# Later modulations summed on VectorE, and neighbourhood queries and keys projected straight into transposed form

## The chip, the cores and the metric

The kernel runs on one core of one Trainium2 chip. The metric is device time in microseconds (us) of one execution, as the median of several runs. One further execution was taken with the hardware profiler; all durations below are from that one.

## The reference, cut to what matters

Two layers of a diffusion backbone work on 1024 latent tokens and 256 context tokens, with a model width of 1024. In each layer a conditioning vector gives shift, scale and gate, the normalised input is modulated and projected once, four branches mix the tokens (A neighbourhood attention, B latent attention, C a recurrent scan, D grouped-query attention), and the branches are merged and projected. Everything is float32. Two places matter here:

```python
def modulation(cond, w_mod, b_mod):
    mod = jax.nn.silu(cond) @ w_mod + b_mod          # (1024,) @ (1024, 3072)
    return jnp.split(mod, 3, axis=-1)                # shift, scale, gate
...
p_lat = (layer_norm(x) * (1.0 + scale) + shift) @ w_in
q, k, v = (split_heads(tt, NA_HEADS) for tt in lat[0:3])    # branch A: 256 columns each
```

The modulation is a vector times a matrix, done for two conditions (latent and context) and for both layers. Branch A's queries and keys are the first 512 columns of the combined projection.

## The kernel before, in words

Data is held in tiles of 128 partitions. The 1280 tokens (256 context, then 1024 latent) make ten token tiles. The modulated input lies transposed in on-chip memory as `xh` and `xl` (width on the partitions, tokens along the free axis), split into a high and a low part of the reduced float type `fp32r`; a float32 product is three `fp32r` products, high x high, high x low and low x high (`mm_a`, `mm_b`, lines 302 to 317). Weights are split in the same way when they are loaded: ScalarE casts the high part (line 263), VectorE subtracts it to get the low part (line 264).

The work of one layer runs in this order: the projection of D (`g_proj`), then two streams woven together, one with the projections of B and A (`m_proj`, `a_proj`) and one with the recurrent branch C (`lru`), then the three attentions (`g_att`, `m_att`, `a_att`) with parts of the gates' products woven in, then `merge`, and then the output projection and the norm (`last`, `outp`). In the profile's names a prefix such as `a_proj__` or `merge__` is the stage, and `wide` is a PSUM tile of three banks that several stages share.

`weave` (line 80) takes generators with a weight each and always advances the one that is least far along for its weight; a generator's `yield` ends one step. A tile framework then sets the final order on each engine's queue and adds the waits, so steps that stand side by side in the code can be interleaved finely. Each engine works its queue in order. SyncE (SP) issues the loads and ScalarE's queue the stores of the projections.

**Modulation.** `modulation` (line 170) loads a piece of `w_mod` of 128 rows and 512 columns (line 185), and multiplies it in float32 with the 128x2 tile `sc` (the two conditions) as the stationary operand and the weights as the moving operand (line 188). The result for 256 or 512 columns lies on two partitions, one group of columns in each of four 32-partition groups of one PSUM bank. At the end ScalarE copies the rows out (line 194), TensorE turns them with small transposes (line 197), and VectorE adds the bias (line 199). The first modulation is needed at the kernel's start. The three later ones (gate of layer 0, shift and scale of layer 1, gate of layer 1; `later_mods`, line 1165) are 64 pieces in all. They are woven with the merge of layer 0 (line 1011): 96 steps of the merge against a weight of 68 for the modulations, which have 67 steps.

**Merge.** For each of the four branches and each of eight output blocks c, `merge` (line 979) forms the gate's product (24 matmuls for a group of tokens, even c) or loads one formed earlier (odd c), applies a sigmoid on ScalarE (line 999), forms the branch's product (6 matmuls into a bank of `wide`), multiplies the two on VectorE (line 1005) and adds the result to the accumulator on VectorE for even c and on GpSimd for odd c (line 1006). In layer 0 there are three groups of tokens (256, 512 and 512), in layer 1 two of 512. The loads of the modulation's pieces use three rotating buffers (tag `q`).

**Projection of A.** `a_steps` (line 801) forms, for each token tile, 24 matmuls with the tokens as the stationary operand and the 512 weight columns as the moving one, so that tokens come out on the partitions. ScalarE copies the two halves out of PSUM, the queries scaled by 0.125 (lines 808 and 809). `put_t` (line 341) then turns the tile with four transposes on TensorE (line 348), splits it into high and low (lines 312 and 313), and stores both in the scratch tensor `qk_a` with two DMAs whose inner runs are 128 tokens (512 bytes). For layer 1 the two context tiles need no queries and use 256 columns. The values follow with weights of their own (lines 819 to 822). The two PSUM banks of `ps_mm` are used in turn.

## Time and profile before

| | |
|---|---|
| median of three runs | 2924.19 us (2923.29 to 2927.37) |
| the profiled execution's own time | 2926.0 us |
| its span, first to last instruction | 2924.2 us |
| TensorE (PE) busy | 2782.2 us, 95% of the span |
| VectorE (DVE) busy | 1503.1 us, 51% |
| ScalarE (ACT) busy | 1219.3 us, 42% |
| GpSimd (POOL) busy | 420.1 us, 14% |
| mean granted TensorE clock | 0.979 of full speed |
| merge of layer 0 with the modulations | about 1085 to 1477 us |
| projection of A woven with the recurrent branch | about 259 to 410 us and 1821 to 1957 us |

An engine's busy time is the time in which at least one of its instructions runs. Matmuls are pipelined, so that a matmul's duration is longer than its distance to the next one; what it costs TensorE is read from the distance between starts. PEld is the load of a stationary operand, which can run beside a matmul.

### The profile page before, as it was taken

How to read it: one execution, taken by the hardware profiler on the slowest of the kernel's cores; microseconds unless marked ns; L12 is line 12 of the kernel's file. 1: busy time of each engine (PE TensorE's matmuls, PEld its weight loads, DVE VectorE, ACT ScalarE, POOL GpSimd, SP SyncE). 2: the span in 40 equal slices, each digit the busy share in tenths (PEclk: the TensorE clock that was granted, in tenths of full speed). 3: DMA queues.
4: the chain of work that ended last, by engine and by line, in shares of the span. 5: the costliest groups of instructions: out<-in, count | busy, mean ns of one | idle time of the engine just before them, and what ended most of it. 6: DMA issues, size and time to landing. Idle time of an engine off the chain costs nothing. (4 is left out here: it accounts for less than half of the span.)

```text
span 2924.2 us, 40179 instructions
## 1 busy us (share of the span) xinstructions
PE 2782.2 (95%) x14458; PEld 2248.4 (77%) x14458; DVE 1503.1 (51%) x3085; ACT 1219.3 (42%) x2617; POOL 420.1 (14%) x507
## 2 busy tenths in 40 slices
PE   7978999999999999999999797999999999999998
PEld 4766788888888887777767586788888888777776
DVE  5645435555455652233358655445555556533357
ACT  4353535445455552222224435535545455522230
POOL 1211011110111100111222121011111111001131
PEclk9988999999999999999999898999999999999999
DMA  7424232222223324333332333342222333222232
GB/s 249 119 66 146 79 103 84 85 85 85 92 86 124 103 94 128 100 121 120 122 89 87 99 102 102 105 122 87 85 88 78 113 115 110 93 87 88 89 113 88
DMA packets 240424, 301.83 MB, mean 103 GB/s; under 512 B 27488, under 2 KB 160096, under 8 KB 240224
## 3 DMA queue, kind: packets, MB, share of 16 engines
q1 hardware_dynamic: 134368, 225.58, 24.5%
q10 hardware_dynamic: 105856, 73.68, 8.1%
q8 instruction: 114, 1.87, 0.3%
q14 instruction: 86, 0.70, 0.1%
HBM read 217.11 MB, written 82.07 MB: 102 GB/s over the span
## 5 line engine op out<-in xcount | busy, mean ns | idle before, releaser
L307 PE MATMUL merge__mm<-xh,merge__whi 128*128 128x512 f32 (+1 forms) x640 | 242.2, 378 | 0.9 <-ACT a_att__tmp L934 0.9
L308 PE MATMUL merge__mm<-xl,merge__whi 128*128 128x512 f32 (+1 forms) x640 | 238.6, 373 | 0.0
L309 PE MATMUL merge__mm<-xh,merge__wlo 128*128 128x512 f32 (+1 forms) x640 | 238.5, 373 | 0.0
L313 DVE TENSOR_TENSOR m_att__pl<-m_att__t,m_att__ph 128x384 fp32r<-128x384 f32 (+1 forms) x248 | 122.0, 508 | 117.5 <-ACT m_att__ph L312 78.8
L1005 DVE TENSOR_TENSOR merge__tmp<-wide,merge__tmp 128x512 f32<-128x512 f32 (+1 forms) x120 | 76.5, 637 | 194.8 <-PE wide L309 173.7
L263 ACT CAST merge__whi<-merge__wraw 128x256 fp32r<-128x256 f32 (+1 forms) x128 | 65.8, 514 | 249.3 <-PE merge__mm L308 172.9
L1006 POOL TENSOR_TENSOR merge__acc<-merge__acc,merge__tmp 128x512 f32<-128x512 f32 (+1 forms) x60 | 79.0, 1317 | 574.8 <-DVE merge__tmp L1005 574.7
L313 DVE TENSOR_TENSOR g_att__pl<-g_att__t,g_att__ph 128x384 fp32r<-128x384 f32 (+1 forms) x228 | 112.8, 515 | 88.3 <-ACT g_att__ph L312 56.0
L312 ACT CAST m_att__ph<-m_att__t 128x384 fp32r<-128x384 f32 (+1 forms) x248 | 105.2, 440 | 115.0 <-PE m_att__t L584 105.3
L307 PEld LDWEIGHTS merge__mm<-xh,merge__whi 128*128 128x128 f32 x640 | 120.2, 188 | 42.8 <-issue 16.5
L264 DVE TENSOR_TENSOR merge__wlo<-merge__wraw,merge__whi 128x256 fp32r<-128x256 f32 (+1 forms) x128 | 72.0, 563 | 131.8 <-ACT merge__whi L263 124.8
L309 PEld LDWEIGHTS merge__mm<-xh,merge__wlo 128*128 128x128 f32 x640 | 120.3, 188 | 23.8 <-issue 0.4
L308 PEld LDWEIGHTS merge__mm<-xl,merge__whi 128*128 128x128 f32 x640 | 120.3, 188 | 22.4
L307 PE MATMUL wide<-merge__uh,merge__whi 128*128 128x256 f32 (+1 forms) x320 | 127.9, 400 | 9.3 <-DVE merge__tmp L1005 6.7
L312 ACT CAST g_att__ph<-g_att__t 128x384 fp32r<-128x384 f32 (+1 forms) x228 | 98.2, 446 | 83.3 <-PE g_att__t L584 78.7
L307 PE MATMUL a_att__mm<-xh,a_att__whi 128*128 128x512 f32 (+1 forms) x320 | 123.7, 387 | 0.0
L641 DVE TENSOR_SCALAR_CACHE_REDUCE g_att__p<-wide 128x1280 f32<-128x1280 f32 (+1 forms) x72 | 98.6, 1369 | 45.9 <-PE wide L639 35.7
L641 DVE TENSOR_SCALAR_CACHE_REDUCE m_att__p<-wide 128x1280 f32<-128x1280 f32 (+1 forms) x72 | 98.7, 1371 | 42.3 <-PE wide L639 41.8
L309 PE MATMUL a_att__mm<-xh,a_att__wlo 128*128 128x512 f32 (+1 forms) x320 | 120.0, 377 | 0.0
L308 PE MATMUL a_att__mm<-xl,a_att__whi 128*128 128x512 f32 (+1 forms) x320 | 120.0, 375 | 0.0
L308 PE MATMUL wide<-merge__ul,merge__whi 128*128 128x256 f32 (+1 forms) x320 | 119.7, 374 | 0.0
L299 PE MATMUL a_proj__mm<-a_proj__whi,xh 128*128 128x256 f32 (+1 forms) x320 | 110.3, 346 | 9.9 <-ACT a_proj__whi L263 9.8
(418 smaller groups left out, 7908.4 us busy)
## 6 DMA issues: line engine op xcount, KB each, us to landing
merge__wraw<-in_w_chunks_dram SPq DMA_DIRECT2D x64, 256.0 KB, 2.9
mod__wm<-in_w_mod_dram SPq DMA_DIRECT2D x64, 256.0 KB, 3.1
g_proj__wm<-in_w_mod_dram SPq DMA_DIRECT2D x16, 512.0 KB, 9.6
a_att__wraw<-in_w_chunks_dram SPq DMA_DIRECT2D x32, 256.0 KB, 2.8
merge__wraw<-in_w_branch_dram SPq DMA_DIRECT2D x64, 128.0 KB, 2.0
merge__tmp<-start__gates SPq DMA_DIRECT2D x32, 256.0 KB, 3.2
merge__tmp<-outp__gates SPq DMA_DIRECT2D x32, 256.0 KB, 3.4
g_att__wraw<-in_w_chunks_dram SPq DMA_DIRECT2D x28, 256.0 KB, 2.7
```

The costliest lines, as they stand in the source:

```text
L263: act.copy(hi[:, :n], raw[:, :n])
L264: (pool if by_pool else dve).tensor_sub(lo[:, :n], raw[:, :n], hi[:, :n])
L299: pe.matmul(ps, xh, wh[:, n0:n1], start=first and k == 0, stop=False)
L307: pe.matmul(ps, wh, xh, start=first and k == 0, stop=False)
L308: pe.matmul(ps, wh, xl, start=False, stop=False)
L309: pe.matmul(ps, wl, xh, start=False, stop=last and k == nk - 1)
L312: act.copy(hi, src)
L313: dve.tensor_sub(lo, src, hi)
L641: dve.tensor_scalar(pt[:, :nk], wide[:, :nk], -scale, None, ALU.mult, ALU.min, accum_out=nb)
L1005: dve.tensor_mul(sgm[:, :g[1]], pb[:, :g[1]], sgm[:, :g[1]])
L1006: (pool if w is None else dve).tensor_add(acc[c][:, gs], acc[c][:, gs], sgm[:, :g[1]])
```

## The change

Two parts, and two weights of `weave` that follow the new numbers of steps.

- `later_mods` calls a new function, `modulation_apart`. For each piece of 128 rows and 512 columns, VectorE multiplies it by the condition's value of each row and adds it to a running sum, once for each of the two conditions (one `tensor_scalar` for the first of eight pieces, `scalar_tensor_tensor` for the others). After eight pieces there are two sums of 128x512. TensorE then adds up the 128 partitions: for each 128 columns a float32 matmul has the sum as its 128x128 stationary operand and one column of -0.5 as its moving operand, which puts the result on the partitions, where it is needed. VectorE multiplies by -2 and adds the bias. The rows, their copies and the small transposes are gone. The running sums lie in buffers of the tags `ph` and `pl`. The steps become 75, the weight 76. The first modulation is as it was.
- `a_steps` makes the 128x128 weight blocks the stationary operand and the tokens the moving one, so that queries and keys come out transposed. ScalarE makes the high part straight from PSUM, VectorE the low part straight from PSUM, and both are stored with inner runs of 256 or 512 tokens. The copies and transposes are gone. There are twelve pieces of work in layer 0 and ten in layer 1; the last two run side by side through the eight weight pairs, as the last two token tiles did before. The weight `W_A` goes from 30 to 32.

```diff
--- before.py
+++ after.py
@@ -34,7 +34,7 @@
 G_LAG = 1
 X_ACT = (0, 2)
 M_ORDER = (2, 3, 1, 0)
-W_A = 30
+W_A = 32
 W_B = 48
 Z_0, GATE_0 = 2, 10
 UNITS = [(2, 3), (5, 3), (8, 2)]
@@ -199,6 +199,39 @@
         dve.tensor_tensor(mc[:, :, :n].rearrange("p s n -> p n s"),
                           tps[:, :2 * n].rearrange("p (n s) -> p n s", s=2),
                           bm[:, :n, None].to_broadcast([128, n, 2]), ALU.add)
+        if n == 16:
+            dve.tensor_scalar(mc[:, :, 8:16], mc[:, :, 8:16], 1.0, None, ALU.add)
+        out["m"] = mc
+        yield
+
+    def raw_w():
+        return tp.tile([128, 512], F32, tag="q", name=nm("wm"), bufs=3)
+
+    def modulation_apart(l, base, ncols, out):
+
+        acc = ps_v.tile([128, 512], F32, tag="pv", name=nm("pm"))
+        n = ncols // 128
+        bm = lc.tile([128, 16], F32, tag="bm", name=nm("bm"))
+        sp.dma_start(bm[:, :n], a["b_mod"][l, :, base // 128:base // 128 + n])
+        for h in range(ncols // 512):
+            sums = [tp.tile([128, 512], F32, tag=tag, name=nm("ms"), bufs=b) for tag, b in (("ph", 3), ("pl", 2))]
+            for k in range(KC):
+                w = raw_w()
+                sp.dma_start(w, a["w_mod"][l, k * 128:(k + 1) * 128, base + h * 512:base + (h + 1) * 512])
+                for s in range(2):
+                    if k == 0:
+                        dve.tensor_scalar(sums[s], w, sc[:, k, s:s + 1], None, ALU.mult)
+                    else:
+                        dve.scalar_tensor_tensor(sums[s], w, sc[:, k, s:s + 1], sums[s], ALU.mult, ALU.add)
+                yield
+            for s in range(2):
+                for c in range(4):
+                    o = s * n + 4 * h + c
+                    pe.matmul(acc[:, o:o + 1], sums[s][:, c * 128:(c + 1) * 128], mhalf[:, 0:1], start=True, stop=True)
+            yield
+        mc = lc.tile([128, 2, 16], F32, tag="modc", name=nm("modc"), bufs=4)
+        dve.scalar_tensor_tensor(mc[:, :, :n], acc[:, :2 * n].rearrange("p (s n) -> p s n", s=2), -2.0,
+                                 bm[:, None, :n].to_broadcast([128, 2, n]), ALU.mult, ALU.add)
         if n == 16:
             dve.tensor_scalar(mc[:, :, 8:16], mc[:, :, 8:16], 1.0, None, ALU.add)
         out["m"] = mc
@@ -800,18 +833,35 @@
 
         def a_steps():
             wa = load_rows(w_in, C_A, 512)
-            prev = None
-            for t, ps in project(wa, lambda t: 0 if t >= q0t else 256, 512):
-                c0 = 0 if t >= q0t else 256
-                y = tmp()
-                if c0 == 0:
-                    act.activation(y[:, :256], ps[:, :256], AF.Copy, scale=0.125)
-                act.copy(y[:, 256:], ps[:, 256:])
-                if prev:
-                    put_t(*prev)
-                prev = qk_a, t, c0 // 128, [y[:, c:c + 128] for c in range(c0, 512, 128)]
+            items = [(c, g) for c in range(4) for g in (qgroups if c < 2 else groups)]
+
+            def part(c, g, ps, ks):
+                xs = xs_g(g)
+                ws = [(wh[:, c * 128:(c + 1) * 128], wl[:, c * 128:(c + 1) * 128]) for wh, wl in wa]
+                mm_b(ps[:, :g[1]], [ws[k] for k in ks], lambda j: xs(ks[j]), ks[0] == 0, ks[-1] == KC - 1)
+
+            def keep(c, g, ps):
+                n, scale = g[1], 0.125 if c < 2 else 1.0
+                hi = tp.tile([128, 512], F32R, tag="ph", name=nm("th"), bufs=3)
+                lo = tp.tile([128, 512], F32R, tag="pl", name=nm("tl"), bufs=2)
+                act.activation(hi[:, :n], ps[:, :n], AF.Copy, scale=scale)
+                dve.scalar_tensor_tensor(lo[:, :n], ps[:, :n], scale, hi[:, :n], ALU.mult, ALU.subtract)
+                for d, s in enumerate((hi, lo)):
+                    act.dma_start(qk_a[d, c, :, g[0]:g[0] + n], s.bitcast(F32)[:, :n])
+
+            for c, g in items[:-2]:
+                ps = mm()
+                part(c, g, ps, list(range(KC)))
+                keep(c, g, ps)
                 yield
-            put_t(*prev)
+
+            last = [(c, g, mm()) for c, g in items[-2:]]
+            for k in range(KC):
+                for c, g, ps in last:
+                    part(c, g, ps, [k])
+            for c, g, ps in last:
+                keep(c, g, ps)
+                yield
             wv = load_rows(w_in, C_AV, 256)
             for t, ps in project(wv, lambda t: 0, 256):
                 put_v(v_a, t, ps[:, :256].rearrange("p (h e) -> p h e", e=64))
@@ -1008,7 +1058,7 @@
 
         for _ in fill["gen"]:
             pass
-        weave((f"merge{l}", merge(), 4 * KC * len(qgroups)), (f"mod{l}", side, 68))
+        weave((f"merge{l}", merge(), 4 * KC * len(qgroups)), (f"mod{l}", side, 76))
 
 
         phase[0] = f"last{l}"
@@ -1159,13 +1209,10 @@
     ctx.push(pools)
     x1 = dr.tile([SEQ, D], F32, name="x1", bufs=1)
 
-    def raw_w():
-        return tp.tile([128, 512], F32, tag="q", name=nm("wm"), bufs=3)
-
     def later_mods():
-        yield from modulation(0, 2048, 1024, gate0, raw_w, 512)
-        yield from modulation(1, 0, 2048, mc1, raw_w, 512)
-        yield from modulation(1, 2048, 1024, gate1, raw_w, 512)
+        yield from modulation_apart(0, 2048, 1024, gate0)
+        yield from modulation_apart(1, 0, 2048, mc1)
+        yield from modulation_apart(1, 2048, 1024, gate1)
 
     def fin0(t, Y, later):
         if t >= CT:
```

## Rows read from the trace of the kernel before

**Rows 1.** The page, part 1: busy time, share of the span, instructions.
```profile
PE 2782.2 (95%) x14458; PEld 2248.4 (77%) x14458; DVE 1503.1 (51%) x3085; ACT 1219.3 (42%) x2617; POOL 420.1 (14%) x507
```

**Rows 2.** Windows: length, busy time of each engine (instructions), granted clock, DMA share, GB/s.
```profile
280.00:360.00 80.00, 80.00 (x389) 65.22 (x388) 31.05 (x34) 40.33 (x62) 0.53 (x1) 0.99 0.28 81
...
1085.00:1475.00 390.00, 385.18 (x1914) 286.72 (x1912) 138.30 (x239) 107.84 (x227) 54.02 (x48) 1.00 0.39 119
1840.00:1960.00 120.00, 115.09 (x636) 97.12 (x637) 48.35 (x64) 52.50 (x88) 0.60 (x2) 0.99 0.33 96
```

**Rows 3.** TensorE's waits from 1060 to 1480 us: total us, times, longest.
```profile
PE wide L307 <- DVE merge__tmp L1005: 3.2, 5, 0.8
PE mod__t L197 <- ACT mod__tmp L194: 1.1, 1, 1.1
...
PE mod__pm L188 <- DMA mod__wm<-in_w_mod_dram: 0.3, 1, 0.3
```

**Rows 4.** Groups of TensorE's instructions, 1085 to 1475 us: busy, mean ns, idle before.
```profile
L188 PE MATMUL mod__pm<-mod__wm,sc 128*2 128x512 f32 x64 | 21.5, 592 | 0.0
...
L188 PE MATMUL mod__pm<-mod__wm,sc 128*2 128x256 f32 x128 | 18.1, 378 | 0.3 <-DMA mod__wm<-in_w_mod_dram 0.3
...
L197 PE MATMUL mod__t<-ident,mod__tmp 2*128 2x2 f32 x28 | 3.1, 203 | 1.2 <-ACT mod__tmp L194 1.1
```

**Rows 5.** Timeline of TensorE in the merge of layer 0: start us, duration us, instruction.
```profile
1233.55 0.28 PE L308 MATMUL wide<-merge__ul,merge__whi 128*128 128x256 f32 x1
1233.67 0.28 PE L309 MATMUL wide<-merge__uh,merge__wlo 128*128 128x256 f32 x1
1233.88 1.02 PE L188 MATMUL mod__pm<-mod__wm,sc 128*2 128x512 f32 x2
1234.83 0.50 PE L307 MATMUL merge__mm<-xh,merge__whi 128*128 128x512 f32 x1
1235.17 0.39 PE L308 MATMUL merge__mm<-xl,merge__whi 128*128 128x512 f32 x1
...
1094.91 0.39 PE L308 MATMUL wide<-merge__ul,merge__whi 128*128 128x512 f32 x1
1095.13 0.39 PE L309 MATMUL wide<-merge__uh,merge__wlo 128*128 128x512 f32 x1
1095.45 0.60 PE L188 MATMUL mod__pm<-mod__wm,sc 128*2 128x256 f32 x4
1095.98 0.50 PE L307 MATMUL merge__mm<-xh,merge__whi 128*128 128x512 f32 x1
1096.32 0.40 PE L308 MATMUL merge__mm<-xl,merge__whi 128*128 128x512 f32 x1
...
1103.14 1.03 PE L188 MATMUL mod__pm<-mod__wm,sc 128*2 128x256 f32 x10
```

**Rows 6.** Groups of VectorE's instructions, whole span: busy, mean ns, idle before.
```profile
L1077 DVE SCALAR_TENSOR_TENSOR outp__Y<-outp__Y,outp__mv,outp__ln_g 128x512 f32<-128x512 f32 x36 | 25.6, 748 | 0.4
...
L313 DVE TENSOR_TENSOR a_proj__tl<-a_proj__t,a_proj__th 128x512 fp32r<-128x512 f32 x18 | 12.3, 683 | 40.6 <-ACT a_proj__th L312 40.5
...
L532 DVE TENSOR_TENSOR_SCAN lru__lruo<-lru__lrug,lru__lruo,lru__lrug 128x1024 f32<-128x1024 f32 x4 | 9.4, 2346 | 0.1
```

**Rows 7.** By tile, stationary loads, matmuls, store issues: ns min/median/max, first and last start.
```profile
L348 PEld LDWEIGHTS a_proj__t<-ident,a_proj__tmp x76: 137/140/226, 278.2 to 1926.9; 128*128 128x128 f32 x76
L348 PE MATMUL a_proj__t<-ident,a_proj__tmp x76: 270/272/477, 278.2 to 1927.1; 128*128 128x128 f32 x76
...
L299 PEld LDWEIGHTS a_proj__mm<-a_proj__whi,xh x320: 186/188/338, 259.3 to 1956.3; 128*128 128x128 f32 x160
...
L355 ACTq DMA_DIRECT2D start__qka<-a_proj__tl x10: 366/366/465, 287.7 to 365.8; - x10
```

**Rows 8.** Timeline of TensorE around four transposes of the projection of A.
```profile
305.93 0.60 PE L348 MATMUL a_proj__t<-ident,a_proj__tmp 128*128 128x128 f32 x4
306.28 0.48 PE L307 MATMUL wide<-xh,lru__whi 128*128 128x512 f32 x1
```

## The prediction

> **What bounds the kernel now.** I read the busy times first: TensorE is at work for 95% of the span, VectorE for 51% [rows 1]. An average over stages is not enough, so the windows come next, cut to the two stretches that the change touches [rows 2]. The merge of layer 0 with the modulations in it has TensorE busy for 385.2 of 390 us and VectorE for 138.3. The projection of A with the recurrent branch has TensorE busy for all of 80 us in layer 0, and for 115.1 of 120 us in layer 1; ScalarE is busy for half of the 80 us. The granted clock in all three is 0.99 or 1.00, so at the upper of the two levels (2.4 GHz), and what is taken off TensorE there is worth its full length. TensorE's waits in the merge say the same from the other side: 3.2 us on VectorE, 1.1 us on the copies of a modulation's rows, 0.3 us on a piece of `w_mod` [rows 3]. Nothing but TensorE's own work ends last there.
>
> **Part 1, what leaves the merge.** The groups show 64 and 128 records for 96 products, so a float32 product is two instructions [rows 4]. Their mean durations must not be added up, since products in different 32-partition groups run beside each other; the cost is in the distances between starts. Undisturbed matmuls are 0.23 us apart at 512 columns and 0.12 at 256 [rows 5]. Around the product of 512 columns at 1233.88, the last matmul before and the second after start 1.50 us apart, where 0.12 + 0.23 would do: 1.15 us. Around the pair of 256 columns at 1095.45 it is 1.19 us in place of 0.46: 0.73 us. A run of ten records takes 1.03 us [rows 5], as long as one product of 512 columns, and I give it 1.15 too. The timeline has 47 such blocks: 21 with 512 columns, 20 short ones and 6 long ones with 256. That is 21 x 1.15 + 20 x 0.73 + 6 x 1.15 = 45.7 us. The small transposes at the end take 3.1 us and the waits before them 1.2 [rows 4]. **TensorE loses 50 us of work.**
>
> **What comes in its place.** There are eight halves of 512 columns (two, four and two), each with eight products of one column: 64 products, 128 instructions. No row shows a product with a full 128x128 float32 stationary operand and one column. From below: four transposes, each with a 128x128 load, take 0.35 us, 0.09 each [rows 8], though the load alone lasts 0.14 and the matmul 0.27 [rows 7]; loads and matmuls overlap. From above: nothing overlaps, and each costs the 0.188 us of a load of the other kind plus 0.272 of the matmul [rows 7], 0.46. A gain is excluded, as they are new. I take 0.12, the distance at which the 256-column matmuls run, each with a load of its own of the 0.188 us kind [rows 5, 7]: 15.4 us. Entering and leaving a block costs 0.2 us (0.09 + 0.11 around 1095.45 [rows 5]), eight times 1.6. Each of the eight blocks also waits for the last sum of VectorE; between nothing and one pair of sums (1.5 us, below) I take 0.4, as a step of the merge lies between them: 3 us of 0 to 12. In all +20 us.
>
> The row on the transposes thus shows stationary loads of the whole array running beside matmuls. The Trainium skill, "TensorE: Matmul & The Clock Gate", Part 3 (The mechanism), states that a stationary load overlaps with matmuls in flight only where the row group differs. By the row the sum stays as above; by the rule the 128 instructions would run one after the other, which is the second rival.
>
> **VectorE** gets 128 instructions of 512 columns. A `scalar_tensor_tensor` on two tiles of on-chip memory takes 0.748 us [rows 6], so a pair (both conditions) 1.5 us and all of them 96 us, added to 138.3 of 390 [rows 2]. That makes about 234 us against the 360 that remain, 65%, so I cost it at nothing on the path. What is queued behind a pair on VectorE are the multiplies that free the banks of `wide` and the low parts of the next weights; if the cover fails, TensorE waits for those, which is the third rival. The bias step reads PSUM once per modulation as before.
>
> **The queue of SP** keeps the 64 loads at the same places. Their buffers are now freed by VectorE, not by TensorE, and behind a load that waits stand the weights, gates and branch outputs of the merge. With three buffers and one piece per 1.3 steps, a pair may run four steps late before the queue stops; I cost it at nothing, as TensorE waited 0.3 us in all for a piece [rows 3].
>
> **Part 2, the projection of A.** 76 transposes leave (40 and 36) at 0.09: -6.7 us. The columns streamed are the same. In layer 0, 96 matmuls of 256 columns replace 48 of 512: 96 x 0.12 - 48 x 0.23 = +0.5 us; in layer 1 the numbers come out equal. ScalarE loses the copies, VectorE keeps one subtraction per piece. The stores go from 40 to 44, at 0.37 us of issue on ScalarE's queue [rows 7]: 1.5 us, behind a ScalarE that is half idle [rows 2]; on the path they would cost those 1.5.
>
> A new wait comes with it. A PSUM bank was free after ScalarE's copies; now VectorE's 0.68 us subtraction [rows 6] has to follow, in a queue where a scan of 2.35 us [rows 6] can stand in front. After a piece of 256 tokens (24 x 0.12 = 2.9 us of cover) the bank of the piece before can be late. There are six such pieces. Bounds: nothing, or the whole 2.9 us each, 17 us. A scan in front gives 2.35 + 0.68 plus a cast, some 0.8 us over the cover; I let it meet half of the six: 2.4 us. The weights of the weave (30 to 32 for 33 to 35 steps in layer 0) keep the pace, so that costs nothing; if it did not, the recurrent branch would run on alone at the end. **Part 2: -4 us.**
>
> **The sum.** -50 + 20 - 4 = -34 us. Against the profiled execution's 2926.0 us that is 2892; that execution lies 1.8 us above the median of the runs, so for the median I forecast **2890 us**. About 0.2% (5.8 us) is what a measurement of this kernel tells from no change.
>
> **The rivals.**
> - *More than counted.* The one-column products run at 0.09 us (13 us with the switches), no block waits, no bank is late: -50 + 13 - 6 = -43, 2881 us. If the idle 4.8 and 4.9 us in the two windows [rows 2] go as well, 2871. For it: the overlap that the transposes show. Against: idle time seldom leaves with work. Chance 0.10.
> - *One-column products in series, slower.* Place: the eight blocks. Price: 128 x 0.46 = 59 us in place of 15. That is 44 us more than in my sum, so -34 becomes +10: 2934 us. It decides from about 0.39 us each, where 128 x 0.27 eats the whole 34. This is what the skill's rule above would do. Against it: 0.09 us apart with 0.14 and 0.27 us long [rows 7, 8]. Chance 0.07.
> - *VectorE sets the pace in the odd blocks.* There a block of the merge is 6 x 0.12 + 12 x 0.23 = 3.5 us of TensorE, while VectorE has three multiplies of up to 0.68 and two pairs of 1.5: 5.0 us. If three banks do not cover the 1.5 us, the 16 odd blocks cost 24 us: 2914 us. Against it: the even blocks, five times as long for TensorE, give VectorE its time back. Chance 0.05.
> - *Banks held in part 2.* All six pieces wait 2.9 us: 17 in place of 2.4 us, 2905 us. For it: VectorE's long operations in that stretch. Chance 0.14.
>
> **How the numbers follow.** My own case has 0.60, with 2881 to 2900 us as its own range (products at 0.09 to 0.15, waits of 0 to 8 us). 0.04 is left for a mixture of the second and third rival that ends within 0.2%. Faster: 0.60 + 0.10 + 0.14 + 0.05 = 0.89; same 0.04; slower 0.07. The range from 2870 to 2908 holds my case, the first and the last rival, 0.84.
>
> **What would show it.** In the merge of layer 0, TensorE's stretch from 1085 to 1475 us should come out some 30 us shorter and still be full, without records of line 188 there, and with 128 short ones about 0.12 us apart; VectorE should be at 60 to 70%. In the projection of A the line of `put_t` should be gone and TensorE's waits on VectorE there stay below 5 us. I am wrong if the one-column records stand 0.3 us or more apart, if TensorE waits for `wide` by more than 15 us in the merge, or if the stretch of A grows.

## The result and the profile after

The changed kernel takes 2891.53 us (median of 4 runs, 2883.76 to 2895.03), the kernel before in the same comparison 2925.01 us (2923.29 to 2927.37): a ratio of 0.9881, 95% interval 0.9858 to 0.9904, so 33.5 us less. The forecast was 2890 us. The profiled execution took 2889.03 us with a span of 2887.3, 37 us less than that of the profiled execution of before.

Part 1 of the page of the changed kernel, to set beside [rows 1]: TensorE lost 41 us of busy time and stayed at 95%, VectorE gained 84.

```profile
PE 2741.0 (95%) x14334; PEld 2252.8 (78%) x14334; DVE 1586.9 (55%) x3215; ACT 1202.9 (42%) x2569; POOL 419.3 (15%) x507
```

To see where the time went I cut both timelines of TensorE at the same work. Each length runs from the first matmul of one stage to the first of the next, in us; the attentions, whose first scores are formed while the projections still run, are counted from their first product with values (`g_att__pv`):

| stage | before | after | change | forecast |
|---|---|---|---|---|
| projections of layer 0 | 388.5 | 376.3 | -12.2 | about -2 |
| attentions of layer 0 | 664.5 | 663.6 | -0.9 | 0 |
| merge of layer 0, modulations and output projection | 548.1 | 524.3 | -23.8 | -30 |
| projections of layer 1 | 338.2 | 335.3 | -2.9 | about -2 |
| attentions of layer 1 | 571.4 | 571.1 | -0.3 | 0 |
| merge and output projection of layer 1 | 375.5 | 378.7 | +3.2 | 0 |

So the total was met, but by two terms that were both off, in opposite directions. The +3.2 in the last stage is not the change's: in the profile of the same kernel with a weave weight of 30 (below) this stage takes 373.9 us. Nor is the -2.9 of layer 1's projections the new projection's: with that part alone they take 337.8 us, with the modulations' part alone 335.3 (both below). Why was not looked into.

Windows of the changed kernel, to set beside [rows 2] (length, then busy time of PE, PEld, DVE, ACT and POOL with instructions, granted clock, DMA share, GB/s):

```profile
270.00:350.00 80.00, 75.17 (x364) 61.26 (x362) 31.22 (x38) 37.26 (x51) 0.00 (x0) 0.98 0.33 110
1070.00:1440.00 370.00, 356.52 (x1826) 295.24 (x1824) 214.38 (x351) 103.47 (x215) 55.20 (x46) 1.00 0.41 123
```

The merge is 30 us shorter in TensorE's work but no longer full: 13.5 us idle in 370, where it was 4.8 in 390 [rows 2]. VectorE is at 58%. TensorE's waits there (1060 to 1445 us; total us, times, longest), to set beside [rows 3]:

```profile
PE wide L340 <- DVE merge__tmp L1055: 10.7, 12, 2.5
PE wide L340 <- DVE merge__acc L1053: 1.5, 3, 1.0
PE wide L340 <- ACT merge__uh L345: 1.5, 2, 1.0
```

All 13.7 us are waits for a bank of `wide` (before: 3.2 on VectorE and 0.8 on ScalarE). None is a wait for the sums. The one-column products themselves, by tile (ns min/median/max, first and last start), and TensorE's timeline around the one block that has 32 of them (start us, duration us):

```profile
L230 PEld LDWEIGHTS mod__pm<-mhalf,mod__ms x128: 187/192/193, 1080.0 to 1440.6; 128*128 128x128 f32 x128
L230 PE MATMUL mod__pm<-mhalf,mod__ms x128: 166/250/251, 1080.2 to 1440.6; 128*128 128x1 f32 x128
...
1241.63 0.40 PE L342 MATMUL merge__mm<-xh,merge__wlo 128*128 128x512 f32 x1
1241.87 3.63 PE L230 MATMUL mod__pm<-mhalf,mod__ms 128*128 128x1 f32 x32
1245.36 0.48 PE L340 MATMUL wide<-merge__uh,merge__whi 128*128 128x512 f32 x1
```

A load lasts 0.192 us and a matmul 0.250, but 32 pairs fit into 1245.36 - 1241.87 = 3.49 us: 0.11 us each, against the 0.12 of the forecast.

**Where the merge waits.** Three of the longest of these waits stand close together: 1.7, 1.3 and 2.5 us, ending at 1180.5, 1184.4 and 1188.7 us. VectorE's timeline just before shows where they begin (in brackets the idle time before an instruction and what ended it):

```profile
1169.48 0.74 DVE L225 SCALAR_TENSOR_TENSOR mod__ms<-mod__wm,sc,mod__ms 128x512 f32<-128x512 f32 x1
1176.41 1.41 DVE L225 SCALAR_TENSOR_TENSOR mod__ms<-mod__wm,sc,mod__ms 128x512 f32<-128x512 f32 x2 [6.20 <-DMA mod__wm<-in_w_mod_dram]
1178.06 1.42 DVE L225 SCALAR_TENSOR_TENSOR mod__ms<-mod__wm,sc,mod__ms 128x512 f32<-128x512 f32 x2 [0.23 <-DMA mod__wm<-in_w_mod_dram]
...
1179.78 0.68 DVE L1055 TENSOR_TENSOR merge__tmp<-wide,merge__tmp 128x512 f32<-128x512 f32 x1
```

VectorE stands 6.2 us in front of a sum whose piece of `w_mod` is late, and behind that sum, in the same queue, stands the product that frees a bank of `wide` (1179.78). TensorE worked on until 1178.9 us and then waited 1.7. Ahead of the late pieces SP's queue had issued the two stores of the gate of layer 0 (timeline of the queue):

```profile
1161.80 1.11 SPq L220 DMA_DIRECT2D mod__wm<-in_w_mod_dram  x2
1162.96 1.06 SPq L1067 DMA_DIRECT2D last__gate<-mod__modc  x2
1164.96 0.38 SPq L220 DMA_DIRECT2D mod__wm<-in_w_mod_dram  x1
...
1183.42 0.33 SPq L311 DMA_DIRECT2D merge__wraw<-in_w_chunks_dram  x1
```

There is a second way from the late piece to a bank. The weight at 1183.42 could be issued only when VectorE had formed the low parts of the weights before it. Their casts ended at 1176.3 and 1179.1 us, but the low parts stood behind the same sums and started at 1183.0. The 2.5 us that end at 1188.7 stand behind the cast and the low part of this weight.

Behind the stores the DMA engines were busy while next to nothing moved (windows: length, PE busy, granted clock, DMA share, GB/s):

```profile
1162.00:1165.00 3.00, 3.00 (x18) 1.00 0.85 235
1165.00:1168.00 3.00, 3.00 (x19) 1.00 0.74 6
1168.00:1171.00 3.00, 3.00 (x14) 1.00 0.78 33
1171.00:1174.00 3.00, 3.00 (x14) 1.00 0.38 17
```

The same stores are in the kernel before, from 1182 us on, and take as long (10.7 us to landing). The windows of before:

```profile
1183.00:1186.00 3.00, 3.00 (x16) 1.00 0.39 10
1186.00:1189.00 3.00, 3.00 (x16) 1.00 0.61 34
1189.00:1192.00 3.00, 3.00 (x15) 1.00 0.63 30
```

TensorE was busy throughout there: it was the only reader of the pieces, and did not reach the late one, which landed at 1194.4 us, 9.1 after its issue. This reading (stores, late piece, VectorE's queue, bank) was formed only after the first nine experiments; the last three test it.

**Where the projection gains.** The kernel before had a stall that the forecast does not name. TensorE's waits of before for the weights of A (240 to 400 us), its timeline (the three longest waits at the values), and the window around them:

```profile
PE a_proj__mm L299 <- ACT a_proj__whi L263: 9.8, 4, 6.2
PE a_proj__mm L300 <- DVE a_proj__wlo L264: 3.0, 1, 3.0
...
362.74 0.38 PE L299 MATMUL a_proj__mm<-a_proj__whi,xh 128*128 128x256 f32 x1 [2.21 <-ACT a_proj__whi L263]
366.13 0.58 PE L300 MATMUL a_proj__mm<-a_proj__wlo,xh 128*128 128x256 f32 x1 [3.00 <-DVE a_proj__wlo L264]
...
374.41 0.39 PE L299 MATMUL a_proj__mm<-a_proj__whi,xh 128*128 128x256 f32 x1 [1.26 <-ACT a_proj__whi L263]
...
360.00:380.00 20.00, 12.63 (x66) 10.58 (x65) 9.61 (x16) 5.31 (x11) 0.00 (x0) 0.83 0.45 125
```

The three in the timeline are at the first products of A's values, which wait for their weights to be split; with a shorter one of 0.2 they come to 6.7 us (the 6.2 is at the first weights of A, earlier), and the granted clock in the window is 0.83. The third and fourth of these weights had landed at 358.9 and 359.3 us. Their casts (line 263) stood in ScalarE's queue behind the copies, casts and stores of the last transposed tiles and started at 362.3. Their low parts (line 264) then stood behind a scan and a product of the recurrent branch in VectorE's queue, until 365.7. The later weights, loaded through the same two buffers, were issued only from 366.1 us on. In the changed kernel TensorE has no wait at these weights; in its place come the bank waits that the forecast priced (waits of TensorE, 240 to 400 us; the last row is at the first weights of A):

```profile
PE a_proj__mm L340 <- DVE a_proj__tl L848: 3.7, 2, 2.9
PE lru__mm L340 <- DVE a_proj__tl L848: 2.4, 1, 2.4
...
PE a_proj__mm L332 <- ACT a_proj__whi L296: 1.1, 1, 1.1
```

### The profile page after: what moved, and what is told of

The parts are those of the page before. It is cut to its first block, busy times and chain, and to the rows that moved or that the text cites. A ratio compares the mean times of both kernels' runs of the same rounds, so it can differ in the third digit from the quotient of the medians.

```text
span 2887.3 us, 40041 instructions
## 1 busy us (share of the span) xinstructions
PE 2741.0 (95%) x14334; PEld 2252.8 (78%) x14334; DVE 1586.9 (55%) x3215; ACT 1202.9 (42%) x2569; POOL 419.3 (15%) x507
## 5 line engine op out<-in xcount | busy, mean ns | idle before, releaser
L342 PE MATMUL wide<-merge__uh,merge__wlo 128*128 128x256 f32 (+1 forms) x320 | 119.2, 372 | 0.0
```

Of the source, the lines that this page charges most:

```text
L342: pe.matmul(ps, wl, xh, start=False, stop=last and k == nk - 1)
```

## The experiments

All were timed beside the kernel before, whose median was 2923.77 us for the first four, 2922.25 for the next four, 2921.56 for the three after them and 2924.88 for the last. "The stage" is merge and output projection of layer 0 in the table above. Lengths of stages come from one profiled execution of each kernel.

### The modulations alone

The kernel before with `modulation_apart` and the side weight of 76:

```diff
-        yield from modulation(0, 2048, 1024, gate0, raw_w, 512)
+        yield from modulation_apart(0, 2048, 1024, gate0)
...
-        weave((f"merge{l}", merge(), 4 * KC * len(qgroups)), (f"mod{l}", side, 68))
+        weave((f"merge{l}", merge(), 4 * KC * len(qgroups)), (f"mod{l}", side, 76))
```

> Only the modulations' part on the kernel before; the projection of A and its weave weight stay as they were. Theory (the trace after, stage by stage: the merge of layer 0 and what follows it came 24 us closer together, the projections of layer 0 12 us, those of layer 1 3 us): about 24 us less than before, 2896 to 2906 us, with TensorE waiting some 10 us for banks of wide in the merge of layer 0. Rival (the prediction's split: 30 us from the modulations): 2895 us or less. Rival (the two parts help each other): less than 15 us gained, 2910 us or more.

Measured: 2896.11 us, ratio 0.9907 (0.9893 to 0.9921); the stage takes 523.3 us, the projections of layer 0 388.2 as before. Part 1 is worth about 27 us by the ratio and 24.8 in its stage, with the same bank waits (9.5 + 0.9 + 0.9 us) as in the changed kernel.

### The projection alone

The kernel before with the new `a_steps` and `W_A = 32`.

> Only the projection of A in transposed form and the weave weight 32; the modulations stay on TensorE. Theory: 12 to 16 us less than before, 2909 to 2913 us, with layer 0's projections 12 us shorter and layer 1's 3 us. Rival (the prediction's split): 4 us less, 2921 us.

Measured: 2910.73 us, ratio 0.996 (0.9947 to 0.9973), about 12 us; projections of layer 0 375.3 us, the stage 547.4. So within the intervals the parts add (27 + 12 against 33.5 by the medians and 37 by the profiles), and part 2 is worth three times the forecast's 4 us. All of it lies in layer 0: the projections of layer 1 take 337.8 us, 0.4 less than before.

### The weight of the weave alone

```diff
-W_A = 30
+W_A = 32
```

> The kernel before with the weave weight W_A at 32 in place of 30 and nothing else. Theory (the end of the projection of B moved 7 us earlier in both layers although none of its instructions changed, so the pace does it): 5 to 9 us less than before, 2916 to 2920 us. Rival (the pace costs nothing, as the prediction said): within 2 us of before, 2923 to 2927 us.

Measured: 2930.29 us, ratio 1.0023 (1.0012 to 1.0035): 6.5 us slower. That the faster pace of A is what gains fell.

### The changed kernel at the old weight

```diff
-W_A = 32
+W_A = 30
```

> The changed kernel with W_A back at 30. Theory (the pace is worth 5 to 9 us): 2896 to 2901 us. Rival (the pace is worth nothing by itself): within 3 us of the changed kernel, 2888 to 2895 us.

Measured: 2888.51 us, ratio 0.9883 (0.9867 to 0.9898), the same as the changed kernel; projections of layer 0 376.6 us. The forecast's zero for the weights holds for the new steps, not for the old ones.

### The sums left out

The changed kernel with 112 of the 128 sums on VectorE left out: the later modulations are then formed from the first of the eight pieces only. The pieces are still loaded.

```diff
-                    else:
-                        dve.scalar_tensor_tensor(sums[s], w, sc[:, k, s:s + 1], sums[s], ALU.mult, ALU.add)
```

> The changed kernel without 112 of VectorE's 128 instructions on the modulations: of each half only the first of eight pieces is multiplied, the other seven are loaded and not used, so the later modulations come out of one eighth of their rows. It prices VectorE's work in the merge of layer 0. Theory (the 12 us that TensorE waits for banks of wide there come from the sums in VectorE's queue; before they were 3 us): those waits fall to about 4 us and the time by 6 to 10 us, 2880 to 2886 us. Rival (the prediction: the sums lie wholly behind TensorE): no change, 2888 to 2895 us, with the waits still at 10 us or more.

Measured: 2891.75 us, ratio 0.9893 (0.988 to 0.9906): no gain over the changed kernel. VectorE's busy time from 1085 to 1430 us falls from 192.2 to 121.6 (windows of the changed kernel and of this one), and TensorE still waits (1060 to 1445 us):

```profile
1085.00:1430.00 345.00, 333.03 (x1702) 275.65 (x1702) 192.21 (x314) 89.93 (x183) 48.86 (x38) 1.00 0.40 118
...
1085.00:1430.00 345.00, 335.19 (x1701) 279.23 (x1700) 121.59 (x217) 86.91 (x174) 41.29 (x34) 0.98 0.36 108
...
PE wide L338 <- DVE merge__tmp L1053: 8.5, 4, 6.2
PE wide L338 <- ACT merge__uh L343: 4.9, 1, 4.9
```

But these are other waits. The ones of 1.7 and 1.3 us around 1182 are gone, and the longest, 6.2 us ending at 1193.1, comes by another way: the pieces that nobody reads are loaded one by one, each as the one before lands, SP's queue stands behind them, and VectorE waits for a weight of the merge that was loaded late:

```profile
1191.43 0.69 DVE L295 TENSOR_TENSOR merge__wlo<-merge__wraw,merge__whi 128x512 fp32r<-128x512 f32 x1 [6.42 <-ACT merge__whi L294]
```

The stage is 530.9 us, 6.6 longer than in the changed kernel, and the granted clock of 0.98 in place of 1.00 over 345 us is worth about as much (0.02 x 345 = 7 us, an estimate). So leaving the sums out also changed the loads, and this run does not say by itself what the sums cost. The next one says more.

### More work for VectorE

Every piece is multiplied by one twice more: 128 instructions. Their median in the trace is 0.42 us, some 54 us in all, and not the 0.48 and 61 of the expectation.

```diff
+                for _ in range(2):
+                    dve.tensor_scalar(w, w, 1.0, None, ALU.mult)
```

> The changed kernel with two more multiplications by 1.0 of each loaded piece on VectorE, in place: 128 instructions of about 0.48 us, 61 us more of VectorE in the merge of layer 0. Theory (VectorE's queue already costs TensorE some 9 us there, in the odd blocks, and more work meets the same gaps): waits for wide grow and the time rises by 5 to 15 us, 2896 to 2907 us. Rival (the cover is thick): within 4 us of the changed kernel. Rival (VectorE becomes the bound of the stage): 25 us or more.

Measured: 2891.32 us, ratio 0.9891 (0.9878 to 0.9903): no change that is clear of the noise. VectorE is then busy for 233.8 of 345 us and the largest wait group is what it was:

```profile
1085.00:1430.00 345.00, 332.07 (x1679) 275.42 (x1678) 233.79 (x422) 87.35 (x175) 44.85 (x36) 0.98 0.40 121
...
PE wide L342 <- DVE merge__tmp L1057: 10.7, 13, 4.1
```

All waits for `wide` come to 14.0 us, against 13.7: VectorE's load does not make them. The stage is 529.9 us, 5.6 longer, at a granted clock of 0.98 in place of 1.00 again; the clock was 0.50 from 1245 to 1250 us, behind the block of 32 short products (see the last section).

### Every product twice

```diff
-                    pe.matmul(acc[:, o:o + 1], sums[s][:, c * 128:(c + 1) * 128], mhalf[:, 0:1], start=True, stop=True)
+                    for r in range(2):
+                        pe.matmul(acc[:, o:o + 1], sums[s][:, c * 128:(c + 1) * 128], mhalf[:, 0:1], start=r == 0, stop=r == 1)
```

(and a factor of -1 in place of -2).

> The changed kernel with each one-column product formed twice and added up in PSUM, and the factor -2 halved to -1: 128 more instructions on TensorE. Theory (a one-column instruction costs what its distance to the next shows, 0.11 us, all of it on the path): 14 us more, 2902 to 2909 us. Rival (loads and matmuls in series, 0.46 us each): 59 us more, about 2950 us. Rival (the waits for banks hide it): within 4 us of the changed kernel.

Measured: 2909.45 us, ratio 0.9952 (0.9938 to 0.9966), 18 us over the changed kernel's median, and the stage 25 us longer (549.4). 128 more instructions at 0.11 are 14 us. The windows around the longest block (64 records from 1249.77 to 1260.77 us, 0.17 us each) show where most of the rest goes, a granted clock at the lower of its two levels (1.2 GHz) while the short products run and after them; from 1085 to 1430 us it is 0.95, against 1.00 in the changed kernel:

```profile
1240.00:1250.00 10.00, 10.00 (x60) 1.00 0.59 191
1250.00:1255.00 5.00, 5.00 (x36) 0.75 0.45 131
1255.00:1260.00 5.00, 5.00 (x25) 0.50 0.50 157
1260.00:1265.00 5.00, 5.00 (x15) 0.50 0.00 0
```

### Only the values' weights moved, in the kernel before

`load_rows` passes `by_pool` on to `load_w`, so that GpSimd and not ScalarE and VectorE splits the weights of A's values.

```diff
-            wv = load_rows(w_in, C_AV, 256)
+            wv = load_rows(w_in, C_AV, 256, True)
```

> The kernel before, with the weights of branch A's values split by GpSimd in place of ScalarE and VectorE, and nothing else. Theory (the chain of copies, transposes, casts and subtractions of the last token tiles stands in ScalarE's queue in front of the casts of these weights, so TensorE waits 7 us for them in layer 0 at about 360 to 376 us and runs at half clock for part of it; the new form of the projection removed that chain): those waits shrink to 2 us or less and the time falls by 5 to 9 us, 2915 to 2919 us. Rival (the waits come from the DMA of the weights): the waits stay and the time stays within 3 us of before.

Measured: 2916.86 us, ratio 0.998 (0.9971 to 0.9989), 5.4 us less; projections of layer 0 380.2 us, 8.3 less. TensorE's waits for these weights are down to 0.2 us; the first row is the first weights of A at the start of the stretch (240 to 400 us), the second a wait for the bank of an earlier tile of values:

```profile
PE a_proj__mm L299 <- ACT a_proj__whi L263: 7.2, 1, 7.2
PE a_proj__mm L299 <- DVE a_proj__vt L313: 3.6, 1, 3.6
...
PE a_proj__mm L300 <- POOL a_proj__wlo L264: 0.2, 1, 0.2
```

This one line, with all transposes in place, gives two thirds of what the new projection gives in layer 0 by the profiles (8.3 of 12.2 us), and a little under half of what it gives in all by the medians (5.4 of about 12).

### The same in the changed kernel

The changed kernel with the weight at 30 and the same line.

> The changed kernel with the weave's weight at 30 and with the weights of A's values split by GpSimd, not by ScalarE and VectorE. My theory: half to two thirds of what part 2 gained in layer 0 was the end of TensorE's waits for these weights (7.2 us before, and the clock's 0.83 after them). In the changed kernel that wait is gone already, so taking it away a second time gives nothing: layer-0 projections at 375 to 378 us, as with the changed kernel at weight 30 (376.6), the whole at 2884 to 2891 us. Rival: the two gains are separate and add: another 6 us off the projections, 370 us, the whole at about 2882 us.

Measured: 2894.29 us, ratio 0.9902 (0.9883 to 0.9921), against 0.9883 without it; projections of layer 0 385.3 us, 8.7 longer. The gains do not add, as my theory had it, but the level was missed: GpSimd needs 0.60 us for a cast and 1.12 for a subtraction, and TensorE now waits for the first of these weights (1.2 + 0.6 us) at a clock of 0.83 from 360 to 380 us, where the same stretch at weight 30 without it is full at 1.00. The rest of the 8.7 us lies ahead of the edited line (200 to 260 us at 0.83, without it 0.89), and why was not found.

### The gate's stores on another queue

```diff
-            sp.dma_start(gd[s].rearrange("(k p) -> p k", p=128), gate["m"][:, s, :KC])
+            act.dma_start(gd[s].rearrange("(k p) -> p k", p=128), gate["m"][:, s, :KC])
```

> The changed kernel with the two small stores of the gate (4 KB each, 9.9 us to landing) issued by ScalarE's queue, not by SP's. Theory one (the stores hold up SP's queue and so the merge's weights around 1170 us): TensorE's waits for the banks of wide in the merge of layer 0 fall from 12 us to 5 or less, the stage from merge to output projection falls from 524 to about 516 us, the whole to 2883 to 2886 us. Theory two (SP's queue is held by the loads of the modulation's pieces, which wait for a buffer that VectorE frees; the stores are only beside it): the waits stay at 8 to 12 us and the stage at 521 to 525 us.

Measured: 2898.96 us, ratio 0.9923 (0.9907 to 0.9939), above the changed kernel, the stage 538.6 us. Theory one fell: TensorE's waits on VectorE for `wide` in the merge did not fall (13.9 us from 1060 to 1450 us, against 12.2 in the changed kernel). They are a little above what theory two allowed, and the stage is far above it. TensorE's and VectorE's waits from 1160 to 1180 us:

```profile
PE wide L340 <- DVE merge__acc L1053: 7.3, 1, 7.3
...
DVE mod__ms L225 <- DMA mod__wm<-in_w_mod_dram: 7.7, 1, 7.7
```

The stores are no longer in SP's queue, and the piece is as late as before; so it is not the queue's order that holds it. The other two stores (gate of layer 1, at 1447 to 1449 us) now run beside the last gate's load of the merge, for which ScalarE waits 9.0 us, and TensorE waits 6.7 us for the product behind it.

### The pieces on another queue

```diff
-                sp.dma_start(w, a["w_mod"][l, k * 128:(k + 1) * 128, base + h * 512:base + (h + 1) * 512])
+                act.dma_start(w, a["w_mod"][l, k * 128:(k + 1) * 128, base + h * 512:base + (h + 1) * 512])
```

> The changed kernel with all 64 loads of the later modulations' pieces issued by ScalarE's queue, not by SP's. Theory two of the run before (SP's queue stands behind pieces that wait for a buffer): the merge's weights are no longer late, TensorE's waits for the banks of wide fall from 12 us to 5 or less and the stage from 524 to about 516 us, the whole to 2883 to 2886 us. Rival: the wait for the buffer now stands ahead of the sigmoids and casts in ScalarE's queue and makes these late in the same way: the stage stays at 521 to 525 us or grows to 530 and more, with TensorE waiting on ScalarE. Theory one (the stores): no change, 521 to 525 us, with the same waits on VectorE as now.

Measured: 2893.75 us, ratio 0.9904 (0.989 to 0.9919), the stage 533.3 us. From 1160 to 1180 us:

```profile
PE wide L340 <- DVE merge__acc L1053: 8.0, 1, 8.0
...
DVE mod__ms L225 <- DMA mod__wm<-in_w_mod_dram: 8.5, 2, 7.3
```

Pieces on ScalarE's queue, stores on SP's, the same wait. That SP's queue stands behind pieces which lack a buffer is not what makes the piece late. The stage is as long as the rival had it, but not by its reason: TensorE waits 1.1 us on ScalarE in the merge, and the granted clock from 1085 to 1430 us is 0.96 in place of 1.00. What both runs leave is the DMA engines themselves: the slowest piece lands 11.1 us after its issue with the stores on ScalarE's queue, 11.8 with the pieces there and 11.4 in the changed kernel, where the median is 2.8 or 2.9.

### The gate stored in runs

Each partition stores its eight values as one run; the order is set right when the output projection reads the gate, with a stride.

```diff
-            sp.dma_start(gd[s].rearrange("(k p) -> p k", p=128), gate["m"][:, s, :KC])
+            sp.dma_start(gd[s].rearrange("(p k) -> p k", k=KC), gate["m"][:, s, :KC])
...
-                    dve.tensor_mul(Y[:, hs], ps, gt[s][:, hs])
+                    gv = gt[s].rearrange("p (q k) -> p k q", k=KC)[:, 4 * h:4 * h + 4, :]
+                    dve.tensor_tensor(Y[:, hs].rearrange("p (k q) -> p k q", k=4),
+                                      ps.rearrange("p (k q) -> p k q", k=4), gv, ALU.mult)
```

> The changed kernel with the gate's scratch tensor in another order: each partition stores its 8 values as one run of 32 bytes, not as 8 elements of 4 bytes, and the output projection's product reads the gate with a stride of 8 elements. The two runs before left TensorE's longest wait where it was (7.3 and 8.0 us), behind a piece that VectorE waits 7.3 to 7.7 us for, while the DMA engines were 63 to 116% busy at 6 to 50 GB/s. Theory: what holds the piece is the store's own time on the DMA engines (9.1 us to landing, whichever queue issues it). With an eighth of the elements it lands in 4 us or less, VectorE's longest wait for a piece near 1170 us falls from 6.2 to 2 us or less, TensorE's waits for wide in the merge from 13.7 to 6 us or less, and the stage from merge to output projection from 524 to about 517 us, the whole to 2884 to 2887 us if the clock in the merge is as in the changed kernel's profile. Rival: the time goes to the store's fixed latency or to the traffic of the pieces themselves: landing stays at 8 us or more and the waits at 10 us or more. A second way to fail: the strided read makes the output projection's products slower than 0.68 us; then VectorE's time there grows and the stage gives back what the merge gains.

Measured: 2894.2 us, ratio 0.9894 (0.9877 to 0.991), the stage 525.3 us: no gain in the whole, for two effects that cancel. In the merge the theory holds, though the waits, 6.9 us in all, are just above the 6 that it named. TensorE's waits (1060 to 1430 us), a window to set beside 0.74 and 6 GB/s, and the store with its median time to landing (KB each, us):

```profile
PE wide L340 <- DVE merge__tmp L1055: 5.1, 8, 0.9
PE wide L340 <- ACT merge__uh L345: 0.9, 2, 0.5
PE wide L340 <- DVE merge__acc L1053: 0.9, 1, 0.9
...
1165.00:1168.00 3.00, 3.00 (x18) 1.00 0.59 168
...
last__gate<-mod__modc SPq DMA_DIRECT2D x2, 4.0 KB, 3.5
```

The store in the changed kernel lands after 9.9 us there, and the slowest piece after 11.4 us, here after 5.5. The merge alone (from its first matmul to the last one of its gates' products) falls from 368.8 to 360.3 us, of which 6.8 are waits. The output projection behind it grows by as much, from 155.5 to 165.0 us, the second way to fail: the strided products last 1.12 us in place of 0.68 (groups of VectorE, 1440 to 1600 us; the last number before the bar is the count, then busy us and mean ns), and TensorE's waits for the banks that they free go from 2.0 to 5.9 us, with the clock at 0.50 from 1515 to 1520 us.

```profile
L1120 DVE TENSOR_TENSOR outp__Y<-wide,outp__gt 128x512 f32<-128x512 f32 x12 | 13.5, 1124 | 21.2 <-PE wide L334 21.2
```

The same group in the changed kernel:

```profile
L1119 DVE TENSOR_TENSOR outp__Y<-wide,outp__gt 128x512 f32<-128x512 f32 x12 | 8.1, 677 | 19.5 <-PE wide L334 19.5
```

A version that stores in runs and reads without a stride was not tried, so whether the whole can be had is open. Nor was the strided read tried alone, so that it makes the whole of the growth is argued and not shown.

## Why the prediction came out, and which of its steps failed

**Bound.** That TensorE's own work ended last in the merge [rows 2, 3] holds: taking it out shortened the stage.

**What leaves and what comes in.** With the stores out of the way, the merge, cut as above, is 388.7 - 360.3 = 28.4 us shorter than before, against 50 - 20 = 30 of the forecast (the last of the small transposes that leave lie behind this cut). The products take 0.11 us in place of 0.12, 14 us in all. The rule by which they would run in series, in the Trainium skill, "TensorE: Matmul & The Clock Gate", Part 3 (The mechanism), is not borne out here: a load of 0.192 and a matmul of 0.250 in series would be 0.44 us, and 0.11 was measured, all on the same rows of the array. The same section also lets a load go ahead of matmuls where it is for the background weight buffer; whether that happens here the traces do not show. The doubled products agree that the price is small, apart from the clock, for which the forecast has no term: the section on the hardware below has what it did.

**The step that failed in part 1** is "I cost it at nothing, as TensorE waited 0.3 us in all for a piece" [rows 3], under the queue of SP. The 0.3 us was read from the engine that used the pieces before. After the change VectorE uses them, and behind the waiting sum stand the products that free `wide` and the low parts of the merge's weights; a like lateness (9.1 us before, 11.4 after), harmless before, is worth 8.5 us. I had named what stands behind a sum on VectorE, but only for VectorE being too busy; the run with 54 us more on VectorE shows that load is not what counts. TensorE's 13.7 us for `wide` stayed just under the 15 that were to show me wrong. The 3 us for waits on the sums came out as 0, and VectorE's 58% is a little under the 60 to 70% of the forecast.

The Trainium skill, "DMA: Bandwidth & Descriptors", section Rules for kernel authors, says that a last dimension that is not contiguous is lowered to one descriptor per element. That agrees with the store of 1024 single values taking 9.9 us to land and the one of 128 runs 3.5.

**The step that failed in part 2** is its sum of -4 us: the measured value is -12 alone. The missing term is a stall behind the edited lines, at the values' weights, whose casts and low parts came late behind other work in ScalarE's and VectorE's queues. It was in TensorE's waits of before (12.8 us on A's weights from 240 to 400 us, 6.7 of them at the values), and I had not asked for the waits of that stretch. Moving only the splitting of those weights gave 8.3 of the 12.2 us in layer 0; that the new projection ends the stall by taking away the tail of ScalarE's work is argued from the timeline, and the two queues were not tested apart. Transposes, columns and stores were not measured one by one; 12.2 - 8.3 = 3.9 us are left for them and the bank waits, where the forecast had about 2 in layer 0. In layer 1 the new projection alone gained 0.4 us. The bank waits were forecast as 2.4 us within 0 to 17 and are 6.1 in layer 0, so the bound of 5 us that I gave for TensorE's waits there was passed. "The weights keep the pace, so that costs nothing" held in the changed kernel.

**The rivals.** Products in series: no. VectorE as the pace: no, by the run with more load on it. Banks held: 8.4 us in both layers (6.1 and 2.3), half of what it would need. More than counted: its 13 us for products was nearly right, but the idle time did not leave, it grew. Part 1 was forecast 3 to 6 us too good (30 against 27 by its own run and 23.8 by its stage), part 2 8 us too poor (4 against 12). That these two errors nearly cancel is luck, and the total looks better than its terms.

## What to carry to other kernels

When an operation moves to another engine, its operands' lateness moves with it: read how long the old engine waited for them, and then what stands behind the new instruction in its queue. Ask for the waits of the whole stretch around an edit, not only of the lines that go; the larger gain can be a stall that the removed work caused further on. And look at windows in which the DMA engines are busy at a few GB/s: two 4 KB stores of single values there made 256 KB loads land after some 11 us in place of 2.8, and neither choice of queue that was tried helped.

## What the runs showed of the hardware that was not expected

- Runs of one-column products lowered TensorE's granted clock although the engine was never idle: 0.50 during and after 64 of them in a row, and the 512-column matmuls behind them started 0.43 us apart in place of 0.23. After a block of 32 it stayed at 1.00 in the profile of the changed kernel and in that with the gate stored in runs, and fell in the six others that have one (to 0.66 from 1245 to 1250 us in the changed kernel at weight 30). The kernels without such products had the clock at 1.00 throughout that merge. In the changed kernel's own profile it fell once, to half from 1189 to 1192 us, behind the 2.5 us wait for `wide`. So one profile of this kernel can differ from another by some 5 us in the merge for the clock alone, which is why stages here are compared together with their clock.
- The profiled execution and the three others of the changed kernel have spans of 2882.0 to 2893.2 us at mean granted clocks of 0.980 to 0.977, the shorter the higher, so at least part of this kernel's spread goes with the clock.
- A product on VectorE with one operand read at a stride of 32 bytes (and all three taken as four runs of 128) took 1.12 us in place of 0.68.
